# A two-layer hybrid trunk on one core: the second layer's pieces put in rounds of 1/32 head, a memset moved to VectorE, and sums of squares moved to another PSUM bank

## The chip, the cores and the metric

The kernel runs on one core of one Trainium2 chip. The metric is device time in microseconds (us) for one launch. PE is TensorE, DVE VectorE, ACT ScalarE, POOL GpSimd, SP the engine that issues the DMAs. Each engine works through its own queue in order.

## The reference, cut to what matters

640 tokens (128 of a prompt, 512 latent) go through two layers of width 1024. Layer A is a gated chunk mixer, layer B a gated DeltaNet scanned in both directions. Cut to layer B, whose order is changed:

```python
qkv, z, ab = split(h @ w_in)                  # per head: k 128, q 128, v 256, z 256 columns
qkv = silu(short_conv(qkv, conv_w))           # 5 taps over the tokens
q = l2norm(q) * 128**-0.5;  k = l2norm(k)     # l2norm needs the sum of squares of each token
# per head, per direction, in chunks:
A   = strict_lower(kb @ k.T * decay)
sol = (I + A)^-1 [v*beta, kb*exp(gcum)]       # triangular solve inside a chunk
S, o = scan over the chunks                   # 128x256 state from chunk to chunk
y = rmsnorm(o_fwd + o_bwd) * norm_g * silu(z)
out = y @ w_out
```

## The kernel before

Tokens are five tiles of 128 (`TT = 5`, tile 0 is the prompt). All large products are done as three products of high and low parts (`mm3`, lines 230 to 232); weights come through the queue `ws`, are cast to a high part on ACT (line 225), and the low part is subtracted on POOL or DVE (line 226).

Layer B goes head by head, eight heads. What it does is written as Python generators, and each `yield` ends a piece:

- `project_head` and `project_z`: 16 pieces each, every piece one `mm3` of 128x320 into a bank of the pool `pp` (two banks), so three matmuls a piece;
- `conv` (lines 834 to 842): on DVE four taps over 642 columns (L837) and a last product (L842), on ACT the first tap and a tanh written over `xp`. `gap` (L848) then sets the two columns between prompt and latent tokens to zero again;
- `post_k`, `post_q`, `post_v`: sums of squares, transposes through `flip` (L235, into the pool `px`, which has one bank), copies out of it on ACT (L901, L927). `post_q` takes q's sums of squares with matmuls against a column of ones (L858, also into `px`), and DVE copies them out (L912);
- `chunk`: the triangular inverse in three groups of token tiles, (0), (1, 4), (2, 3), started 0.09 of a head apart, 40 pieces each. Six levels of doubling: L1006 on PE, a masked product Y on DVE (L1011), L1017 and L1018 on PE, a copy TU on ACT (L1021). Then `U16`, half of it written by POOL (L1030), is transposed by L1037, refined through L1046, L1047, and used by L1053. The result goes through L1063 to G. All small products share the pool `pt` (three banks);
- `scan`: the recurrence, L1101 then L1104 and L1109 on DVE, L1114 and L1115, L1129, with the pool `ps` (two banks);
- `norm_o`, `gate_z` (transposes of o by `flip` into `px`, product on DVE L1196) and `residual` (lines 682 to 690: a load, three POOL products and a store, in windows of four heads).

`stages` gives each generator a stretch of time, in heads. `turns` spreads its pieces evenly over that stretch and sorts all pieces by their time; the program is written in that order. From time 0 on, where the first scan begins, PE and SP keep the written order (`manual_schedule`); the orders of DVE, ACT and POOL are made by a scheduler from the same pieces. A tile of PSUM whose bank is still being read makes the next writer of that bank wait.

Of the kernel before, what the change touches and what calls it, by code (L numbers as in the profile page):

```python
# [13 lines left out]
P = 128  # L14
# [4 lines left out]
NPR = 128  # L19
NSA = 512  # L20
NT = NPR + NSA
TT = NT // P
# [51 lines left out]
def tok(c):  # L74

    s = 0 if c == 0 else 2 + c * P
    return slice(s, s + P)


ZW, ZPOS = (1, 2, 3, 4, 5, 6, 6, 6), 0  # L80
START = 2, 0.3, 1
PIECES = {"scan": 24, "chunk": 40, "norm_o": 4, "gate_z": 4, "conv": 8, "post_k": 13,
          "post_q": 7, "post_v": 5, "gates": 7, "gates_e": 26, "residual": 16}


def stages():
# [5 lines left out]
    for w in range(-2, H + 1):  # L92
        at = lambda d: 0 <= w + d < H
        add = lambda f, arg, t0, t1, k=None: parts.append((f, arg, k or PIECES[f], w + t0, w + t1))
        slots = [("head", w + 2, q) for q in range(4) if at(2)]
        slots[ZPOS:ZPOS] = [("z", h, q) for h in range(H) if ZW[h] == w for q in (4, 5)]
        start = START[w + 2] if w + 2 < len(START) else 0
        wide = (n - start) / len(slots) if slots else 0
# [27 lines left out]

def turns(parts):

    return sorted((f + (k + 0.5) / n * (t - f), i) for i, (_, _, n, f, t) in enumerate(parts)
                  for k in range(n))  # L130


class Stream:
# [69 lines left out]
class Trunk:  # L203
# [8 lines left out]
    def t(self, pool, shape, dt, tag, bufs=None):  # L212
        kw = {} if bufs is None else {"bufs": bufs}
        return pool.tile(shape, dt, tag=tag, name=self.name(tag), **kw)
# [407 lines left out]
    def layer_b(self):  # L622
# [6 lines left out]
        with contextlib.ExitStack() as banks, pool("b_c") as bc:  # L629
# [19 lines left out]
            with pool("b_1", 1) as self.b1, pool("b_2", 2) as self.b2, contextlib.ExitStack() as self.last:  # L649
                self.bg = self.last.enter_context(pool("b_g", 1))  # L650
                self.xp = [t(self.b1, [P, NT + 6], F32, f"xp{i}") for i in range(2)]
                for x in self.xp:
                    nc.gpsimd.memset(x, 0.0)
                self.nxp = 0
                self.kq, self.ch, self.oo, self.ssq, self.acc, self.zz = {}, {}, {}, {}, {}, {}
                parts = stages()
                gens = [getattr(self, f)(*arg) for f, arg, *_ in parts]
                order = turns(parts)
                manual = [when >= 0 for when, _ in order].index(True)
                for _, i in order[:manual]:  # L660
                    next(gens[i], None)

                with tc.manual_schedule(engines=MANUAL):
                    for _, i in order[manual:]:
                        next(gens[i], None)
                    for g in gens:
                        for _ in g:
                            pass
                self.last.close()
                self.out_b()  # L670
# [174 lines left out]
        yield  # L845

    def gap(self, xp):
        self.nc.gpsimd.memset(xp[:, 2 + NPR : 4 + NPR], 0.0)  # L848

    def squares(self, s, xp, dst):  # L850

# [52 lines left out]
    def post_q(self, h, q):  # L904

        nc, t = self.nc, self.t
        s, xp = self.acc[h, q]
        kq = self.kq[h]
        ssq = self.ssq[h] = t(self.b1, [P, TT], F32, "ssq", bufs=5)
        px = self.bank("px", [P, 4, P])  # L910
        yield from self.squares(s, xp, px[:, 0, 0:TT])
        nc.vector.tensor_copy(ssq, px[:, 0, 0:TT])  # L912
        yield
        s4 = s[:, tok(1).start : tok(4).stop].rearrange("p (c n) -> p c n", c=4)
        nc.scalar.copy(kq[:, 1:TT, 1, :], s4)
        yield
        nc.scalar.copy(kq[:, 0, 1, :], s[:, tok(0)])
        yield
# [484 lines left out]
```

## Time and profile before

| | |
|---|---|
| times of three runs | 1387.90, 1391.88 and 1399.34 us, median 1391.88 |
| the profiled execution | 1387.0 us, span 1385.2 us |
| PE busy | 1296.3 us, 94% of the span |
| DVE, ACT, POOL busy | 869.8, 578.4 and 548.0 us |
| mean granted PE clock | 0.977 |

Layer A and its output product take the span up to about 545 us. Layer B's early projections and gates follow to about 690 us, the steady heads to about 1180 us, then the last head and the output product. A busy PE row counts a matmul's whole stay in the array, and rows overlap; where start times stand in a timeline, the distance from start to start is the matmul's price. In a row `<-` names the releaser of the wait, as the profile infers it.

### The profile page before, as it was taken

Reading aid. Unit: us, or ns where it says so; the run is one execution under the profiler, and the core shown is the slowest. Engines: PE = TensorE matmul, PEld = TensorE weight load, DVE = VectorE, ACT = ScalarE, POOL = GpSimd, SP = SyncE. Lnnn points to the kernel's source line nnn. Section 1 sums busy time; section 2 is a strip of 40 time slices with the busy share of each in tenths; the row PEclk is TensorE's granted clock in tenths of the full one; section 3 lists DMA queues with packets and bytes.
Section 4 is the critical chain, followed back from the end, with each engine's and each line's share of the span. In section 5 each row is a group of like instructions: output and inputs, shape, how many; then the busy total and the mean of one; then the engine's idle time right before and its main releaser. Section 6 shows DMA issues by size and latency. Waiting matters only on the chain.

```text
span 1385.2 us, 22850 instructions
## 1 busy us (share of the span) xinstructions
PE 1296.3 (94%) x8773; PEld 1148.0 (83%) x8773; DVE 869.8 (63%) x1572; ACT 578.4 (42%) x1352; POOL 548.0 (40%) x592
## 2 busy tenths in 40 slices
PE   7999999999999998888899999899898998999995
PEld 4688999999997876778788989899898988987784
DVE  4654744444448646987777676687766777455447
ACT  2333522223224325656454554545446354343320
POOL 0221322122126315453546354474655656431014
PEclk9999999999999999999999999999999999999998
DMA  8522233333336232231322224233342432435731
GB/s 329 164 71 82 96 128 117 134 122 122 124 127 252 76 103 108 79 114 57 103 72 69 93 72 136 60 108 109 90 139 68 130 120 66 151 131 159 258 97 77
DMA packets 90255, 163.18 MB, mean 118 GB/s; under 512 B 9089, under 2 KB 55457, under 8 KB 90017
## 3 DMA queue, kind: packets, MB, share of 16 engines
q1 hardware_dynamic: 90144, 161.71, 35.4%
q8 instruction: 69, 1.13, 0.3%
q14 instruction: 42, 0.34, 0.1%
HBM read 135.97 MB, written 25.71 MB: 117 GB/s over the span
## 4 chain that ended last, share of the span: by engine, by line
PE 65%; DVE 14%; issue 6%; POOL 5%; DMA 4%; ACT 4%; SPq 0%; POOLq 0%; DVEq 0%; ACTq 0%
PE pacc L230 10%; PE pacc L232 10%; PE pacc L231 10%; PE pp L230 6%; PE pp L231 6%; PE pp L232 6%; DVE cacc L837 3%; PE ps L1101 3%; DVE M L971 3%; POOL rs L243 2%; PE ps L1115 2%; PE pmod L302 2%; PE pacc L452 1%; POOL wlo L226 1%; DMA lnb<-in_ln 1%
## 5 line engine op out<-in xcount | busy, mean ns | idle before, releaser
L226 POOL TENSOR_TENSOR wlo<-wraw,whi 128x256 fp32r<-128x256 f32 (+1 forms) x193 | 200.3, 1057 | 232.4 <-ACT whi L225 213.5
L230 PE MATMUL pp<-hThi,whi 128*128 128x320 f32 (+1 forms) x784 | 284.7, 363 | 1.5 <-ACT hThi L225 1.5
L231 PE MATMUL pp<-hThi,wlo 128*128 128x320 f32 (+1 forms) x784 | 247.2, 315 | 0.0
L232 PE MATMUL pp<-hTlo,whi 128*128 128x320 f32 (+1 forms) x784 | 246.8, 315 | 0.2 <-DVE hTlo L226 0.2
L225 ACT CAST whi<-wraw 128x256 fp32r<-128x256 f32 (+1 forms) x268 | 147.5, 594 | 101.6 <-PE pacc L231 66.5
L837 DVE SCALAR_TENSOR_TENSOR cacc<-xp,convw,cacc 128x642 f32<-128x642 f32 x128 | 144.2, 1127 | 24.5 <-ACT cacc L834 22.8
L230 PE MATMUL pacc<-hThi,whi 128*128 128x320 f32 x512 | 159.6, 312 | 0.0
L232 PE MATMUL pacc<-hTlo,whi 128*128 128x320 f32 x512 | 158.3, 309 | 0.0
L231 PE MATMUL pacc<-hThi,wlo 128*128 128x320 f32 x512 | 158.2, 309 | 0.0
L230 PEld LDWEIGHTS pp<-hThi,whi 128*128 128x128 f32 (+1 forms) x784 | 151.1, 193 | 5.8 <-ACT hThi L225 1.8
L231 PEld LDWEIGHTS pp<-hThi,wlo 128*128 128x128 f32 (+1 forms) x784 | 150.9, 192 | 4.5
L232 PEld LDWEIGHTS pp<-hTlo,whi 128*128 128x128 f32 (+1 forms) x784 | 149.7, 191 | 1.7 <-DVE hTlo L226 0.6
L226 DVE TENSOR_TENSOR wlo<-wraw,whi 128x1024 fp32r<-128x1024 f32 (+1 forms) x75 | 87.6, 1173 | 69.6 <-ACT whi L225 69.4
L230 PEld LDWEIGHTS pacc<-hThi,whi 128*128 128x128 f32 x512 | 96.1, 188 | 3.1 <-issue 2.2
L231 PEld LDWEIGHTS pacc<-hThi,wlo 128*128 128x128 f32 x512 | 96.1, 188 | 0.0
L232 PEld LDWEIGHTS pacc<-hTlo,whi 128*128 128x128 f32 x512 | 96.1, 188 | 0.0
L243 POOL TENSOR_TENSOR rs<-ve,mhalf 128x1 f32<-128x1 f32 (+2 forms) x39 | 39.6, 1017 | 141.0 <-DVE ve L241 141.0
L251 POOL TENSOR_SCALAR gsq<-gsq 128x320 f32<-128x320 f32 (+1 forms) x52 | 27.7, 532 | 136.9 <-ACT gsq L250 135.9
L252 DVE TENSOR_TENSOR gsq<-pacc,gsq 128x320 f32<-128x320 f32 (+1 forms) x52 | 29.1, 564 | 73.0 <-POOL gsq L251 72.9
L230 PE MATMUL pacc<-whi,hThi 128*128 128x512 f32 x160 | 63.2, 406 | 8.2 <-ACT whi L225 4.8
L250 ACT ACTIVATE gsq<-pacc 128x320 f32<-128x320 f32 (+1 forms) x52 | 25.7, 498 | 106.9 <-PE pacc L232 102.9
L1101 PE MATMUL ps<-S,kq 128*128 128x256 f32 x256 | 64.2, 390 | 4.6 <-DVE o L1129 4.6
(323 smaller groups left out, 3001.1 us busy)
## 6 DMA issues: line engine op xcount, KB each, us to landing
wraw<-in_w_b SPq DMA_DIRECT2D x48, 512.0 KB
wraw<-in_w_ada SPq DMA_DIRECT2D x37, 512.0 KB
wraw<-in_w_uz SPq DMA_DIRECT2D x32, 512.0 KB
v<-kvd SPq DMA_DIRECT2D x72, 128.0 KB
wraw<-in_a_wo SPq DMA_DIRECT2D x16, 512.0 KB
wraw<-in_b_wo SPq DMA_DIRECT2D x16, 512.0 KB
kvd<-nat SPq DMA_DIRECT2D x24, 320.0 KB
cacc<-yd SPq DMA_DIRECT2D x24, 320.0 KB
```

Of the source, the lines that this page charges most:

```text
L225: self.nc.scalar.copy(hi, src)
L226: (e_lo or self.nc.vector).tensor_tensor(lo, src, f32(hi), op=ALU.subtract)
L230: mm(out, l_hi, r_hi, start=start, stop=False)
L231: mm(out, l_lo, r_hi, start=False, stop=False)
L232: mm(out, l_hi, r_lo, start=False, stop=stop)
L243: nc.gpsimd.tensor_tensor(r, ve, self.mhalf[:, 0:n], op=ALU.pow)
L252: nc.vector.tensor_tensor(sq, u, sq, op=ALU.mult)
L302: nc.tensor.matmul(ps[32 * j : 32 * j + 32, 0:256], self.sil[:, 4 * i + j, :], w[:, j, :], start=(i == 0), stop=(i == 1), tile_position=(0 ...
L837: nc.vector.scalar_tensor_tensor(acc, xp[:, i : i + PADN], w[:, i : i + 1], acc, op0=ALU.mult, op1=ALU.add)
L971: nc.vector.scalar_tensor_tensor(M[:, i, 1 + d], pe[:, i], self.beta[:, c, d, h : h + 1], m[:, 2 + d], op0=ALU.mult, op1=ALU.mult)
L1101: nc.tensor.matmul(p[:, q], kq[:, c, q, :], S, start=True, stop=True)
L1115: nc.tensor.matmul(p[:, 1], G[:, 1 + d], r, start=True, stop=True)
```

## The change

`turns` cuts time into rounds of 1/32 head. Within a round the projections come first, then `chunk`, then everything else, then `scan`; inside each class the old order holds. Times below 0 keep the old order. Second, `gap` is issued on VectorE instead of GpSimd. Third, `post_q` puts its sums of squares into a bank of `pt` instead of `px`. Nothing is computed differently.

```diff
+ROUNDS = 32
 ...
 def turns(parts):
-    return sorted((f + (k + 0.5) / n * (t - f), i) for i, (_, _, n, f, t) in enumerate(parts)
-                  for k in range(n))
+    rank = lambda f: 0 if f.startswith("project_") else {"chunk": 1, "scan": 3}.get(f, 2)
+    order = [(f + (k + 0.5) / n * (t - f), i) for i, (_, _, n, f, t) in enumerate(parts) for k in range(n)]
+    return sorted(order, key=lambda x: (x[0] * ROUNDS // 1, rank(parts[x[1]][0]), x) if x[0] >= 0 else (x[0] * ROUNDS,))
 ...
     def gap(self, xp):
-        self.nc.gpsimd.memset(xp[:, 2 + NPR : 4 + NPR], 0.0)
+        self.nc.vector.memset(xp[:, 2 + NPR : 4 + NPR], 0.0)
 ...
-        px = self.bank("px", [P, 4, P])
-        yield from self.squares(s, xp, px[:, 0, 0:TT])
-        nc.vector.tensor_copy(ssq, px[:, 0, 0:TT])
+        ps = self.bank("pt", [P, TT])
+        yield from self.squares(s, xp, ps)
+        nc.vector.tensor_copy(ssq, ps)
```

Line numbers of the changed kernel are higher by 3 from `turns` on (L858 is L861 there, L235 is L238).

The first place is PE's queue at the sums of squares of a middle head: `L858` and the projections up to `L1053`. Before:

```order
L235 MATMUL px_9331<-ident_487,nat_9072 128x128
L858 MATMUL px_9282<-ones_4857,xp_763_4879 128x1 x5
L230 MATMUL pp_9267<-hThi_64,whi_9179 128x320
L231 MATMUL pp_9267<-hThi_64,wlo_9180 128x320
L232 MATMUL pp_9267<-hTlo_65,whi_9179 128x320
L230 MATMUL pp_9267<-hThi_64,whi_9179 128x320
L231 MATMUL pp_9267<-hThi_64,wlo_9180 128x320
L232 MATMUL pp_9267<-hTlo_65,whi_9179 128x320
L1053 LDWEIGHTS U_1684_9220
```

The same place in the changed kernel; nine of the twelve projection matmuls are shown, and three more and then `L1056` (L1053 before) follow:

```order
L238 MATMUL px_9338<-ident_487,nat_9091 128x128
L861 MATMUL pt_9308<-ones_4857,xp_763_4879 128x1 x5
L233 MATMUL pp_9243<-hThi_64,whi_9169 128x320
L234 MATMUL pp_9243<-hThi_64,wlo_9170 128x320
L235 MATMUL pp_9243<-hTlo_65,whi_9169 128x320
L233 MATMUL pp_9351<-hThi_64,whi_9169 128x320
L234 MATMUL pp_9351<-hThi_64,wlo_9170 128x320
L235 MATMUL pp_9351<-hTlo_65,whi_9169 128x320
L233 MATMUL pp_9351<-hThi_64,whi_9169 128x320
L234 MATMUL pp_9351<-hThi_64,wlo_9170 128x320
L235 MATMUL pp_9351<-hTlo_65,whi_9169 128x320
```

The sums now go to `pt`, and twelve projection matmuls instead of six stand between them and `L1053`.

The second place is PE's queue where `gate_z` begins, in the changed kernel: the last transpose of `post_v` (out of `cacc`) and the first four of `gate_z` (out of `o`), both into the one bank of `px`.

```order
L234 MATMUL pp_8628<-hThi_64,wlo_8446 128x320
L235 MATMUL pp_8628<-hTlo_65,whi_8445 128x320
L238 MATMUL px_8654<-ident_487,cacc_8361 128x128
L238 MATMUL px_8656<-ident_487,o_7483 128x128
L238 MATMUL px_8656<-ident_487,o_7686 128x128
L238 MATMUL px_8656<-ident_487,o_7690 128x128
L238 MATMUL px_8656<-ident_487,o_7487 128x128
L233 MATMUL pp_8628<-hThi_64,whi_8445 128x320
```

Before, six projection matmuls stood between the two; now none does. The same happens at six heads.

The third place is POOL's queue at `U16` of the third group, with the semaphores waited for. Before:

```order
L226 TENSOR_TENSOR wlo_9382<-wraw_9065,whi_9381 128x256 [waits Activation_49] x3
L682 TENSOR_SCALAR lnb_9479<-lnb_9479 128x512 [waits DMAHW6_49]
L687 TENSOR_TENSOR rn_9482<-rn_9482,lnb_9479 128x256 [waits DMAHW7_49,Pool_49]
L689 TENSOR_TENSOR rn_9482<-rn_9482,lnb_9479 128x256 [waits Pool_49]
L1030 TENSOR_SCALAR U_1711_9334<-TU_1580_8715 128x2x2x64 [waits PE_49]
L848 MEMSET xp_762_4878 128x2 [waits DVE_49]
```

And in the changed kernel:

```order
L229 TENSOR_TENSOR wlo_9362<-wraw_9059,whi_9361 128x256 [waits Activation_49] x3
L685 TENSOR_SCALAR lnb_9505<-lnb_9505 128x512 [waits DMAHW6_49]
L690 TENSOR_TENSOR rn_9508<-rn_9508,lnb_9505 128x256 [waits DMAHW7_49,Pool_49]
L692 TENSOR_TENSOR rn_9508<-rn_9508,lnb_9505 128x256 [waits Pool_49]
L1033 TENSOR_SCALAR U_1710_9334<-TU_1580_8715 128x2x2x64 [waits PE_49]
```

The memset behind `U16` has gone; the residual's three products ahead of it have stayed.

Over the stretch from the first scan to the last, PE changes from a small 16-bit matmul (L991 to L1053) to a projection 118 times before and 54 times now, and from any small matmul to a projection 290 times before and 198 times now.

## The prediction

> **What bounds the kernel now.** I read the page's first part, then the busy time by stage, since layer A is not touched.
>
> ```profile
> PE 1296.3 (94%) x8773; PEld 1148.0 (83%) x8773; DVE 869.8 (63%) x1572; ACT 578.4 (42%) x1352; POOL 548.0 (40%) x592
> core 0: us, PE busy (x) PEld busy (x) DVE busy (x) ACT busy (x) POOL busy (x), PEclk, DMA share, GB/s
> 690.00:1180.00 490.00, 465.59 (x3621) 431.40 (x3620) 354.98 (x688) 248.85 (x703) 275.75 (x340) 0.97 0.31 96
> ```
>
> PE is the bound. In the steady heads, 690 to 1180 us, it is idle for 490 - 465.6 = 24.4 us, and its clock is 0.97. The stage before 690 is written in the old order, so what rounds can win lies in these 24.4 us, in the clock, and in how cheaply PE goes from one kind of matmul to the next. PE's waits there, in total, with their number and the longest, are:
>
> ```profile
> PE pt L1037 <- POOL xp L848: 12.2, 6, 2.9
> PE ps L1101 <- DVE o L1129: 4.6, 6, 1.2
> PE px L858 <- ACT kq L901: 4.1, 5, 1.1
> PE pt L1018 <- DVE Y L1011: 2.2, 5, 0.4
> PE pt L1017 <- DVE Y L1011: 1.1, 1, 1.1
> ```
>
> Two of them carry names that the change touches: L858 waits for its bank in `px`, and L1037 waits for what looks like the memset. PE's timeline at one head shows both, and what follows them:
>
> ```profile
> 805.12 0.27 PE L235 MATMUL px<-ident,nat 128*128 128x128 f32 x1
> 805.89 1.28 PE L858 MATMUL px<-ones,xp 128*128 128x1 f32 x10 [0.50 <-ACT kq L901]
> ...
> 807.99 0.40 PE L1053 MATMUL pt<-R,U 128*128 128x128 f16 x4
> 809.54 0.61 PE L1037 MATMUL pt<-id,U 128*128 128x128 f16 x4 [1.15 <-POOL xp L848]
> 810.32 0.47 PE L231 MATMUL pp<-hThi,wlo 128*128 128x320 f32 x1
> 810.59 0.47 PE L232 MATMUL pp<-hTlo,whi 128*128 128x320 f32 x1
> ```
>
> After the two waits the projections start 0.27 us apart.
>
> **Memset.** L1037 does not wait for the memset. The U16 of the third group may be written only when L1053 of the second group has read the old one (one buffer), L1037 is the next thing in PE's queue, and POOL does this between the two:
>
> ```profile
> 890.23 0.62 POOL L682 TENSOR_SCALAR lnb<-lnb 128x512 f32<-128x512 f32 x1 [1.24 <-DMA lnb<-in_ln]
> 890.93 1.17 POOL L687 TENSOR_TENSOR rn<-rn,lnb 128x256 f32<-128x256 f32 x1
> 892.18 0.72 POOL L689 TENSOR_TENSOR rn<-rn,lnb 128x256 f32<-128x256 f32 x1
> 892.99 0.40 POOL L1030 TENSOR_SCALAR U<-TU 128x256 f16<-128x256 f16 x1
> 893.33 0.10 POOL L848 MEMSET xp<- 128x2 f32 x1
> ```
>
> U16 (L1030) ends at 893.39, the memset at 893.43: the memset stands behind what PE needs. In four heads the residual's products, held by a load, are ahead; in the others U16 alone. The order shows all of this unchanged but for the memset, so I leave the 12.2 us in place: term **0**, ends -0.6 (0.1 us at each of six) and -12.2. On DVE the memset's nearest rows are POOL's own and DVE's copy of five columns:
>
> ```profile
> L848 POOL MEMSET xp<- 128x2 f32 x24 | 2.4, 99 | 11.3 <-DVE cacc L842 9.4 <-ACT xp L854 1.9
> L912 DVE COPY ssq<-px 128x5 f32<-128x5 f32 x6 | 1.0, 160 | 1.8 <-PE px L858 1.7
> L837 DVE SCALAR_TENSOR_TENSOR cacc<-xp,convw,cacc 128x642 f32<-128x642 f32 x96 | 108.7, 1132 | 23.4 <-ACT cacc L834 21.8
> ```
>
> There are 32 of them (three convolutions and one square a head): at most 32 x 0.16 = 5.1 us of DVE, which has 490 - 355 = 135 us free in the steady heads. After a convolution the memset follows DVE's own L842 and waits for nobody; after `squares` it waits for ACT's square, and behind it stands L912's copy, which needs that square too. Term 0, at worst 5.1 us if DVE's cover were gone. POOL loses a wait (11.3 us of idling before L848) that no PE row names except as above.
>
> **Sums of squares to `pt`.** L858 no longer waits for L901's copy: 4.1 us in five heads. But in the four heads with a residual PE then only comes sooner to L1037, whose wait POOL ends: there the gain is taken back. I keep the one without, 0.5 us (the row at 805.89). Term **-0.5**, ends 0 and -4.1. In `pt` the sums hold one of three banks until DVE's L912; behind L858 twelve projection matmuls follow in the middle heads before `pt` is used again, and L912 takes 0.16 us.
>
> **Rounds: a new neighbour in `px`.** At six heads `gate_z`'s first transposes now stand directly behind `post_v`'s last, in the same bank, and wait for ACT's copy out of it. This is not in the trace; the nearest thing is L858 above, a transpose, an ACT copy of 128x128, then the next writer:
>
> ```profile
> L901 ACT COPY kq<-px 128x128 f32<-128x128 f32 x6 | 1.5, 246 | 1.3 <-PE px L235 1.3
> L927 ACT ACTIVATE nat<-px 128x128 f32<-128x128 f32 x12 | 3.2, 267 | 0.0
> ```
>
> The copies are alike (246 and 267 ns), so I take the mean wait of L858, 4.1 / 5 = 0.82 us: six times **+4.9 us**, ends 0 (PE held up by something else anyway) and 6 x 1.1 = 6.6. One wait in `px` is exchanged for another.
>
> **Rounds: fewer changes of kind.** What a change costs stands in PE's timeline:
>
> ```profile
> 800.38 0.28 PE L1006 MATMUL pt<-TU,A 128*128 128x64 f16 x4
> 800.49 0.39 PE L230 MATMUL pp<-hThi,whi 128*128 128x320 f32 x1
> 800.72 0.31 PE L231 MATMUL pp<-hThi,wlo 128*128 128x320 f32 x1
> 800.87 0.31 PE L232 MATMUL pp<-hTlo,whi 128*128 128x320 f32 x1
> ```
>
> The first projection behind 16-bit matmuls holds the next for 0.23 us, the second for 0.15: 0.08 us a change. There are 118 - 54 = 64 fewer: **-5.1 us**. Behind 32-bit matmuls the first holds longer still,
>
> ```profile
> 827.09 0.59 PE L1114 MATMUL ps<-v,G 128*128 128x256 f32 x2
> 827.52 0.59 PE L1115 MATMUL ps<-v,G 128*128 128x256 f32 x2
> 827.77 0.49 PE L230 MATMUL pp<-hThi,whi 128*128 128x320 f32 x1
> 828.10 0.31 PE L231 MATMUL pp<-hThi,wlo 128*128 128x320 f32 x1
> ```
>
> 0.33 us, but nothing is lost: two such matmuls take 0.43 us from start to start (827.09 to 827.52), so the L1115 would reach 827.95; L230 begins 0.18 before that and ends its hold 0.15 after it, as long as any projection. Ends: 0, and all 290 - 198 = 92 changes at 0.33 - 0.15 = 0.18, -16.6 us.
>
> **Rounds: shorter cover.** A chunk's PE step needs DVE's or ACT's answer to the one before. Projections between them hide it. The longest such run grows, but the shortest shrinks: where L1018 follows L1006 at the last level, twelve projections and four transposes stood between, now six projections, 6 x 0.15 = 0.9 us. Counting the order with such start-to-start times, no step of `chunk` behind the first scans had a cover under 1.5 us; now 20 places do. What the answer takes when DVE is free:
>
> ```profile
> 867.24 0.47 PE L1006 MATMUL pt<-TU,A 128*128 128x64 f16 x10
> 867.51 0.95 DVE L1011 TENSOR_TENSOR Y<-pt,wm 128x128 f16<-128x128 f32 x3 [0.51 <-PE pt L1006]
> 869.83 0.23 PE L1018 MATMUL pt<-TU,Y 128*128 128x128 f16 x1
> ```
>
> All three Y are there at 868.46; L1006's ten starts (0.3 us), a change of kind (0.08) and six projections would bring PE to about 868.5. It just fits. Term 0; the upper end is the slower rival. The waits of L1101 and L1018 (6.8 us) I leave: ends -6.8 and 0.
>
> **The clock.** The granted clock was half of full in these stretches:
>
> ```profile
> 809.60:812.80 3.20, 3.20 (x14) 3.19 (x15) 0.22 (x1) 0.58 (x1) 1.16 (x1) 0.50 0.03 5
> 891.50:898.10 6.60, 4.65 (x18) 4.30 (x19) 1.04 (x3) 0.58 (x1) 2.92 (x5) 0.50 0.01 2
> ...
> sum 26.40, PE 20.39 PEld 19.50 DVE 3.04 ACT 3.82 POOL 11.15; mean PE 4.08 PEld 3.90 DVE 0.61 ACT 0.76 POOL 2.23
> ```
>
> Five heads, 20.4 us of PE at half speed, at most 10.2 us lost. Each stretch begins in the wait of L1037 or at its end, behind L858's one-column matmuls. At 809.6 three light pieces led up to it, waits of 0.50 and 1.15 us and L858's 1.28. The change puts six more projections (0.88 us) between L858 and L1037, but lets L1037's wait grow by what L858 lost. Term 0, ends -10.2 and +5.
>
> The Trainium skill bears on this ("TensorE: Matmul & The Clock Gate", Part 1): PE is taken to half clock after about 3.4 us without work, and gaps below that are harmless. By that rule no wait here would cost clock, the term would be 0 at both ends and the sum -0.7 us whatever the waits do. The trace disagrees: half clock followed waits of 0.50 and 1.15 us; by it the sum can lie between -10.9 and +4.3 us by this term alone.
>
> **The sum**: -0.5 + 4.9 - 5.1 = -0.7 us. The profiled execution took 1387.0 us, less than all three runs shown; the middle of the four times is (1387.9 + 1391.9) / 2 = 1389.9. I set the sum against that: **1389 us**. Against 1387.0 it would be 1386.
>
> **The rivals.** Differences under 1% (13.9 us) are about what a measurement of this kernel cannot tell from none.
>
> - *Slower, by late answers.* At the 20 places DVE takes one more L837 (1.13 us) before Y or T32, with some 0.3 us of slack: 20 x 0.8 = +16 us, 1405. It decides when DVE still has such a tap in hand as L1006 ends. For it: DVE is 72% busy there, and L1018 already waits 0.4 us in five heads. Against it: the free DVE in the rows at 867. Chance 0.20.
> - *Faster, by the clock.* If L858 and L1037 are now far enough apart that the clock holds, and their waits do not merge, 10.2 us and L858's other 3.6 go: 1389 - 14 = 1375. For it, the first head, where L1037 waited with no L858 close by:
>
> ```profile
> 729.35 0.34 PE L1037 MATMUL pt<-id,U 128*128 128x128 f16 x3 [0.88 <-POOL xp L848]
> ```
>
> ```profile
> 728.00:735.00 7.00, 6.12 (x50) 5.65 (x49) 3.46 (x8) 4.32 (x15) 1.97 (x4) 1.00 0.00 0
> ```
>
> The clock stayed whole. Against it: 0.88 us is short, and with the residual the longest wait is 2.9. Chance 0.15.
> - *Faster, by the memset.* Were the profile's name right and L1037 held by L848, 12.2 and 10.2 us would go: 1366. Against it stands the POOL order. Chance 0.07.
> - *Faster, by the changes of kind at their upper end*: -16.6 + 4.9 - 0.5 = -12, with a wait of L1018 or two gone 1375. Chance 0.05.
>
> **How the numbers follow.** My forecast, within 1% with everything nearly cancelling, has 0.53. Slower by over 1% has the first rival's 0.20 and 0.01 for a clock that falls more often; faster by over 1% the other three less a part that stays inside, 0.26. The range runs from just inside the clock rival with the waits of L1018 gone (1389 - 14 - 5 = 1370) to the slower rival with a little clock (1406).
>
> **What would show it.** L858's wait gone from PE's waits; a new wait of a transpose L238 on ACT's copy L930, six times, near 0.8 us; L1040 (L1037 before) still waiting for POOL 12 us or more; PE busy in the steady heads lower by about 5 us; half-clock stretches still once a head behind L1040. Wrong would be: L1040's wait much shorter, no half clock in the middle heads, or waits of L1020 and L1021 on DVE above 5 us in sum.

## The result, and the profile after

The changed kernel took 1429.49 us (median of four, 1429.37 to 1434.58) against 1391.85 us before: ratio 1.0271, 95% interval 1.0247 to 1.0295. It is **2.7% slower, 38 us**. The forecast was 1389 us with 1406 as the upper end, so it was wrong. The profiled execution took 1429.5 us with a span of 1427.7, 42.5 us longer than the span of before; its page has:

```profile
PE 1313.2 (92%) x8773; PEld 1161.4 (81%) x8773; DVE 870.0 (61%) x1604; ACT 574.9 (40%) x1352; POOL 549.5 (38%) x560
```

PE is busy 17 us longer, with the same 8773 matmuls, and still fills less of the span. A fair comparison takes the same work on both sides: from the 529th matmul of layer B's projections to the 2257th, which is six heads; 38.3 of the 42.5 us lie in it. The busy time for that stretch, first of before, then of after:

```profile
703.28:1206.10 502.82, 478.41 (x3727) 443.38 (x3726) 358.13 (x701) 250.90 (x709) 282.07 (x350) 0.97 0.33 102
```

```profile
709.28:1250.40 541.12, 493.04 (x3727) 455.15 (x3726) 354.94 (x721) 248.67 (x712) 284.55 (x325) 0.94 0.30 93
```

The columns are the stretch, its length, and the busy time of PE, PE's loads, DVE, ACT and POOL, then PE's granted clock. PE is idle for 48.1 us instead of 24.4, and the clock falls from 0.97 to 0.94. The stretches of half clock (a granted clock of 0.50) in these heads are eleven instead of five; here are the third and the sum over all, then the sum over the five of before:

```profile
849.38:856.21 6.83, 4.95 (x14) 3.96 (x14) 4.68 (x13) 0.47 (x1) 4.69 (x6) 0.50 0.03 11
...
sum 64.86, PE 55.70 PEld 48.59 DVE 24.86 ACT 8.32 POOL 33.13; mean PE 5.06 PEld 4.42 DVE 2.26 ACT 0.76 POOL 3.01
```

```profile
sum 27.31, PE 20.95 PEld 19.99 DVE 3.45 ACT 4.00 POOL 11.48; mean PE 4.19 PEld 4.00 DVE 0.69 ACT 0.80 POOL 2.30
```

55.7 us of PE at half speed lose 27.9 us; before it was 20.95 us and 10.5. (The prediction's 20.4 and 10.2 came from windows a little narrower than the stretches.) So the 38.3 us of these six heads split, with rounding, into 23.7 us of new idling, 17.4 us of clock, and -2.7 us that is left over (465.2 instead of 467.9 us of work at full clock). The waits of PE from 690 to 1230 us:

```profile
PE pt L1009 <- DVE TU L996: 24.7, 6, 4.3
PE pt L1040 <- POOL U L1033: 13.7, 6, 5.0
PE px L238 <- ACT kq L904: 4.3, 2, 2.2
PE pt L1040 <- ACT U L1030: 2.4, 5, 0.5
PE px L238 <- ACT nat L930: 2.2, 6, 0.4
PE pt L1020 <- DVE Y L1014: 0.7, 1, 0.7
```

One row carries nearly all: once a head the first level of group (0)'s inverse, L1009, waits 4.1 us for DVE's product TU. Before, the same step, L1006, had no such wait in these heads. PE's timeline at one head of after, without the projections that stand between the rows:

```profile
844.23 0.28 PE L994 MATMUL pt<-id,A 128*128 128x128 f16 x2
...
845.29 0.60 PE L238 MATMUL px<-ident,cacc 128*128 128x128 f32 x4
...
846.90 0.31 PE L235 MATMUL pp<-hTlo,whi 128*128 128x320 f32 x1
851.26 0.26 PE L1009 MATMUL pt<-TU,A 128*128 128x64 f16 x2 [4.05 <-DVE TU L996]
```

and the same head before:

```profile
829.72 0.28 PE L991 MATMUL pt<-id,A 128*128 128x128 f16 x2
...
831.65 1.03 PE L1101 MATMUL ps<-S,kq 128*128 128x256 f32 x4
833.40 1.13 PE L1101 MATMUL ps<-S,kq 128*128 128x256 f32 x4 [0.72 <-DVE o L1129]
...
834.82 0.23 PE L1006 MATMUL pt<-TU,A 128*128 128x64 f16 x2
```

Before, scan's L1101 stood between L991 and L1006, and the second four of it waited for DVE's `o`. After, `chunk` has a rank ahead of `scan`, so L1009 comes first and the L1104 behind it. From L991 to L1006 PE took 5.10 us; from L994 to the end of the last projection ahead of L1009 it takes 847.21 - 844.23 = 2.98. What DVE does meanwhile, after and then before:

```profile
844.85 1.77 DVE L966 SCALAR_TENSOR_TENSOR A<-ge,beta,masks 128x128 f32<-128x128 f32 x4
846.53 4.01 DVE L974 SCALAR_TENSOR_TENSOR M<-pe,beta,masks 128x128 f32<-128x128 f32 x4
850.47 0.41 DVE L1132 TENSOR_TENSOR o<-o,ps 128x256 f32<-128x256 f32 x1
850.80 0.41 DVE L996 TENSOR_TENSOR TU<-pt,wm 128x256 f16<-128x256 f32 x1
```

```profile
829.09 1.12 DVE L963 SCALAR_TENSOR_TENSOR A<-ge,beta,masks 128x128 f32<-128x128 f32 x4
830.13 2.88 DVE L971 SCALAR_TENSOR_TENSOR M<-pe,beta,masks 128x128 f32<-128x128 f32 x3
832.94 0.41 DVE L1129 TENSOR_TENSOR o<-o,ps 128x256 f32<-128x256 f32 x1
833.27 0.91 DVE L971 SCALAR_TENSOR_TENSOR M<-pe,beta,masks 128x128 f32<-128x128 f32 x1
834.10 0.41 DVE L993 TENSOR_TENSOR TU<-pt,wm 128x256 f16<-128x256 f32 x1
```

TU itself takes 0.4 us; ahead of it stand A and M of the **next** group, 6 us. TU ended 4.79 us behind the start of L991 before, and ends 6.98 us behind L994 after, because DVE begins A 1.25 us later against PE (why was not followed), and A and M take 0.9 us longer. The cover is 2.1 us shorter, the answer 2.2 us later, and 0.3 us was spare: 4.0 us.

Much of M's 4.0 us goes together with POOL's work in the same stretch, first below. Four of the same products later in the same trace, where POOL is idle, are in the second fence:

```profile
846.70 1.31 POOL L980 TENSOR_TENSOR A<-A,ident 128x512 f16<-128x512 f32 x1 [0.22 <-DVE A L966]
848.09 1.15 POOL L982 TENSOR_TENSOR L<-A,A 128x512 f16<-128x512 f32 x1
849.20 1.20 POOL L997 TENSOR_TENSOR TU<-A,wm 128x512 f16<-128x512 f16 x1
```

```profile
923.79 1.14 DVE L974 SCALAR_TENSOR_TENSOR M<-pe,beta,masks 128x128 f32<-128x128 f32 x4 [1.04 <-PE pt L1066]
```

The first of the four at 846.53 takes 0.26 us from start to start; the three behind it take 1.28, 1.23 and 1.16, and each ends 0.14 or 0.15 us behind one of POOL's three products; it is so in all six heads. So of DVE's queue ahead of TU some 2.9 us go with POOL's work at the same time. It was nearly so before (3.8 us for the four, at 830.13 and 833.27). No run moved POOL's products, so this is read from the traces alone.

### The profile page after: what moved, and what is told of

Its sections match the earlier page's. It is cut to its first block, busy times and chain, and to the rows that moved or that the text cites. A ratio compares the mean times of both kernels' runs of the same rounds, so it can differ in the third digit from the quotient of the medians.

```text
span 1427.7 us, 22870 instructions
## 1 busy us (share of the span) xinstructions
PE 1313.2 (92%) x8773; PEld 1161.4 (81%) x8773; DVE 870.0 (61%) x1604; ACT 574.9 (40%) x1352; POOL 549.5 (38%) x560
## 4 chain that ended last, share of the span: by engine, by line
PE 66%; DVE 17%; issue 5%; POOL 4%; DMA 4%; ACT 2%; SPq 0%; POOLq 0%; DVEq 0%; ACTq 0%
PE pacc L233 10%; PE pacc L235 10%; PE pacc L234 10%; PE pp L233 6%; PE pp L235 6%; PE pp L234 6%; DVE cacc L840 4%; PE ps L1104 4%; DVE M L974 3%; POOL rs L246 2%; PE pmod L305 2%; DVE A L966 1%; PE pacc L455 1%; PE ps L1118 1%; PE px L238 1%
## 5 line engine op out<-in xcount | busy, mean ns | idle before, releaser
L229 POOL TENSOR_TENSOR wlo<-wraw,whi 128x256 fp32r<-128x256 f32 (+1 forms) x193 | 205.1, 1081 | 226.5 <-ACT whi L228 202.9
L233 PE MATMUL pp<-hThi,whi 128*128 128x320 f32 (+1 forms) x784 | 275.5, 351 | 1.5 <-ACT hThi L228 1.5
L235 PE MATMUL pp<-hTlo,whi 128*128 128x320 f32 (+1 forms) x784 | 248.0, 316 | 0.2 <-DVE hTlo L229 0.2
L235 PE MATMUL pacc<-hTlo,whi 128*128 128x320 f32 x512 | 158.3, 309 | 0.0
L235 PEld LDWEIGHTS pp<-hTlo,whi 128*128 128x128 f32 (+1 forms) x784 | 150.6, 192 | 1.7 <-DVE hTlo L229 0.6
L840 DVE SCALAR_TENSOR_TENSOR cacc<-xp,convw,cacc 128x642 f32<-128x642 f32 x128 | 140.2, 1095 | 16.5 <-ACT cacc L837 15.4
L235 PEld LDWEIGHTS pacc<-hTlo,whi 128*128 128x128 f32 x512 | 96.1, 188 | 0.0
L1104 PE MATMUL ps<-S,kq 128*128 128x256 f32 x256 | 70.7, 425 | 0.0
```

The lines of the kernel that those rows point to most:

```text
L229: (e_lo or self.nc.vector).tensor_tensor(lo, src, f32(hi), op=ALU.subtract)
L233: mm(out, l_hi, r_hi, start=start, stop=False)
L235: mm(out, l_hi, r_lo, start=False, stop=stop)
L840: nc.vector.scalar_tensor_tensor(acc, xp[:, i : i + PADN], w[:, i : i + 1], acc, op0=ALU.mult, op1=ALU.add)
L1104: nc.tensor.matmul(p[:, q], kq[:, c, q, :], S, start=True, stop=True)
```

## The experiments

Each is the changed kernel with one edit, unless it says otherwise. "Six heads" means the stretch above, split as above.

### The rounds, or the rest

`e1_no_rounds` takes `ROUNDS` and the new `turns` out:

```diff
-    order = [... rank(...) ...]
+    return sorted((f + (k + 0.5) / n * (t - f), i) for i, ...)
```

> The change without its rounds: the memset on VectorE and the sums of squares in pt, in the old order. Theory A (the rounds cost the 38 us: in them chunk stands ahead of scan, L1009 loses the cover that scan's L1104 gave it): within 5 us of before, 1387 to 1397, L858 (L861 after) waits for nothing, no wait of L1009 above 1 us, half clock once a head. Theory B (the memset in VectorE's queue makes VectorE late for TU): a good part of the 38 us stays, 1405 to 1430, with L1009 waiting for VectorE.

`e2_rounds_only` is the kernel before with the new `turns` alone.

> The rounds alone: memset on GpSimd, sums of squares in px. Theory A: all of the slowdown is here, 1425 to 1440 (the sums in px wait for kq's copy besides, up to 4 us), L1009 waits some 4 us once a head. Theory B: near before, 1390 to 1400.

Measured: 1390.61 us, ratio 0.9991 (0.9973 to 1.0009), and 1434.74 us, ratio 1.0309 (1.0288 to 1.0331). The cost is the rounds'. Without them the two other edits cost nothing, and the memset's name is gone from the wait while the wait stays (`e1_no_rounds`):

```profile
PE pt L1037 <- POOL U L1030: 16.7, 6, 4.2
PE ps L1101 <- DVE o L1129: 5.5, 6, 1.2
```

What L858 no longer waits there, L1037 waits longer (17.8 instead of 12.8 us, with ACT's part). With the rounds alone it is the other way round: L861 (L858 before) waits 12.2 us, far more than the 4 us expected, and L1040 6.1 us.

### The ranks of chunk and scan

```diff
-    {"chunk": 1, "scan": 3}.get(f, 2)
+    {"chunk": 3, "scan": 1}.get(f, 2)
```

> The change with scan ahead of the others and chunk last within a round (ranks 1 and 3 exchanged), so that scan's four L1104 stand between L994 and the first L1009 of the last group once more. Theory A: the waits of L1009 fall from 24.7 us to under 8 us (four L1104 give 1.6 us of the 4.1 and hold PE until DVE's o besides), and with them the half clock behind them: 1390 to 1405. Rival C (any order with nine projections in a row at the head of a round starves the chunk's steps): the waits move to other steps of chunk, 1415 to 1430.

Measured: 1390.15 us, ratio 0.9999 (0.9974 to 1.0024). Theory A. Rounds of 1/32 with nine projections at their head do not cost 38 us; the order of `chunk` and `scan` in them does. L1009's wait is down to a third (8.5 us, where under 8 was expected), and what the prediction feared shows in its place, L1021 behind a late Y:

```profile
PE pt L1021 <- DVE Y L1014: 9.5, 7, 1.9
PE pt L1009 <- DVE TU L996: 8.5, 6, 2.0
```

`e6_flat` keeps the projections first and drops the other ranks:

```diff
-    rank = lambda f: 0 if f.startswith("project_") else {"chunk": 1, "scan": 3}.get(f, 2)
+    rank = lambda f: 0 if f.startswith("project_") else 1
```

> Rounds with the projections first and all else in its old order (no ranks for chunk and scan). Theory A: L1104 stands ahead of the first L1009 again; time near the version with scan first, 1385 to 1397, with waits of L1009 of 1.0 to 1.5 us a head. Rival C: 1405 or more.

Measured: 1382.29 us, ratio 0.9938 (0.9914 to 0.9962): 0.6% faster than before, below what theory A gave. In the six heads (494.4 us) PE idles 24.8 us, as before; half clock costs 3.4 instead of 10.5 us, and there is 1.8 us less of work. So "projections first" alone was a small gain, also against the 1390.61 us without rounds, and the ranks behind it threw it away.

### One piece moved

`e9_one_piece` moves the single piece with that L1009, and with it its Y on DVE, behind its round's scan; L956 and everything else stay.

```diff
+    late = lambda i, k: parts[i][0] == "chunk" and parts[i][1][1] == GROUPS[0] and k in (8, 9)
-    rank = lambda f: 0 if ...
+    rank = lambda i, k: 4 if late(i, k) else 0 if ...
```

> The change with one piece of its order moved, once a head: the first L1009 of group (0) stands behind the L956 and the four scan matmuls L1104 of its round instead of ahead of them (on VectorE its Y moves with it); everything else stays. Theory A (this one place holds the cost): the wait goes from 4.1 us to about 4.1 - 0.9 - 1.9 = 1.3 us a head, 17 us of waiting gone, and with it the half clock behind it (about 2.5 us of loss a head in the last four heads): 25 to 32 us gone, 1397 to 1405. Rival C (the waits come with the rounds wherever chunk stands): under 10 us gone.

Measured: 1402.83 us, ratio 1.0104 (1.0048 to 1.0160), 27 us less than the change. One piece a head holds that much. But not for the reason given: the waiting did not go, it was divided (lines are higher by 3 again):

```profile
839.17 1.13 PE L1107 MATMUL ps<-S,kq 128*128 128x256 f32 x4 [2.03 <-DVE o L1135]
840.13 0.22 PE L1012 MATMUL pt<-TU,A 128*128 128x64 f16 x2
...
842.81 0.22 PE L1023 MATMUL pt<-Y,TU 128*128 128x64 f16 x2 [1.06 <-DVE Y L1017]
```

PE now meets the same stretch of DVE at scan's `o`, 2.0 us, and at Y, 1.1 us. In the six heads idling falls only from 48.1 to 41.1 us; the loss by clock falls from 27.9 to 12.8. Two short waits, 3.1 us together, cost far less clock than the long one of 4.1 us.

### DVE's queue

`e8_M_short` leaves PE's order alone and shortens what stands ahead of TU: one product in place of four for the second group. It leaves the factor beta out, so what this kernel computes is not the layer any more; its time alone counts here.

```diff
+        if cs == GROUPS[1]:
+            nc.vector.tensor_tensor(M[:, :, 1:3], pe[...], m[...], op=ALU.mult)
...
+                if cs != GROUPS[1]:
                     nc.vector.scalar_tensor_tensor(M[:, i, 1 + d], pe[:, i], self.beta[...], ...)
```

> The change with the second group's four products into M on VectorE (L974, 1.0 us each, the last thing ahead of TU in VectorE's queue) replaced by one product of 128x512 that leaves the factor beta out; PE's order is the change's. Theory A' (the wait of L1009 is VectorE's queue, not TU's own work and not GpSimd): one product of some 1.2 us instead of four of 4.0: the wait falls by 2.8 us a head to about 1.3 (17 us), and with the clock 22 to 30 us are gone, 1399 to 1408. Rival E (TU waits for PE's L994 or for the bank, VectorE's queue only stands beside it): the wait stays over 3 us and the time over 1420.

Measured: 1392.54 us, ratio 1.0007 (0.9986 to 1.0028). The whole loss is gone, more than expected, since the product took 0.68 us and not 1.2:

```profile
833.57 1.80 DVE L966 SCALAR_TENSOR_TENSOR A<-ge,beta,masks 128x128 f32<-128x128 f32 x4
835.29 0.68 DVE L973 TENSOR_TENSOR M<-pe,masks 128x512 f32<-128x512 f32 x1
835.90 0.41 DVE L1136 TENSOR_TENSOR o<-o,ps 128x256 f32<-128x256 f32 x1
836.23 0.41 DVE L1000 TENSOR_TENSOR TU<-pt,wm 128x256 f16<-128x256 f32 x1
```

```profile
PE pt L1013 <- DVE TU L1000: 4.8, 6, 1.0
```

A is as slow as in the change; M alone is short, and L1009 (L1013 here) waits 0.8 us. In the six heads 17.2 us of idling and 15.6 us of clock go. Of the 4.1 us of waiting, 3.3 are these M products in DVE's queue. Whether by their own work or by POOL's products between them the run does not tell apart, since one product leaves fewer places for POOL's to come between.

`e4_M_later` was meant as the same test by order: the four M products written behind TU.

> The change with chunk's products into M (L974, four of 1.0 us on VectorE) written behind the product into TU (L996) instead of ahead of it; PE's order is as in the change. Theory A in its form 'L1009 waits for VectorE's queue, of which M is 4 us': the wait of L1009 goes from 4.1 us a head to about 0, with the half clock behind it (3.4 to 5 us of PE at half speed, 1.7 to 2.5 us lost a head): 30 to 40 us gone, 1390 to 1400. Rival D (VectorE's backlog only moves on to Y L1014 and r L1107, for which L1020 and L1118 wait): 1415 to 1430 with new waits of L1020 or L1117.

Measured: 1416.01 us, ratio 1.0174 (1.0157 to 1.0191), with 20.6 us of waiting at L1009 left. The time is in theory D's range, but the new waits that D names are not there (0.7 us at L1020). The edit did not have the effect it was meant for: DVE's order is made by a scheduler, and that put M ahead of TU again (L998 is M, L994 TU here):

```profile
836.75 1.86 DVE L998 SCALAR_TENSOR_TENSOR M<-pe,beta,masks 128x128 f32<-128x128 f32 x2
838.53 0.41 DVE L1134 TENSOR_TENSOR o<-o,ps 128x256 f32<-128x256 f32 x1
838.87 2.13 DVE L998 SCALAR_TENSOR_TENSOR M<-pe,beta,masks 128x128 f32<-128x128 f32 x2
840.92 0.41 DVE L994 TENSOR_TENSOR TU<-pt,wm 128x256 f16<-128x256 f32 x1
```

Where its 13 us come from was not followed further; in the six heads there is 4.7 us less idling and 6.2 us less loss by clock.

### The clock by itself

`e7_filler` fills the wait with useless work and takes no wait away:

```diff
+            if l == 1 and nt == 1 and h > 1:
+                for _ in range(17):
+                    nc.tensor.matmul(fill, self.id16, self.wm[:, 0:2]..., start=True, stop=True)
```

> The change with 17 useless 16-bit matmuls of 512 columns (the identity against a mask) ahead of the first L1009 of group (0) in the six steady heads, into the bank that L1009 then writes; nothing else moves on PE or VectorE. An estimate from L994's 128 columns in 0.056 us: 0.22 us each, 3.8 us of work in the 4.1 us of waiting. Theory F (the half clock behind L1009 follows PE's idleness there, and costs 10 us or so by itself): the wait is filled, the clock holds behind it, and the time falls by 8 to 14 us, 1416 to 1421, though PE has 22 us more to do. Rival G (the half clock has another cause, the light 16-bit pieces or VectorE's lateness): the time stays within 3 us of the change's 1429, and the half clock behind L1009 too.

Measured: 1411.91 us, ratio 1.0156 (1.0118 to 1.0194): **17.6 us faster than the change with 22 us more work for PE.** The stretch about the filled wait runs at full clock here, as in all six heads, where the change had half:

```profile
841.80 3.84 PE L1011 MATMUL pt<-wm,id 128*128 128x512 f16 x17
846.05 0.22 PE L1014 MATMUL pt<-TU,A 128*128 128x64 f16 x2 [0.41 <-DVE TU L997]
```

```profile
845.50:852.50 7.00, 6.59 (x44) 5.80 (x42) 4.78 (x14) 1.52 (x4) 5.77 (x7) 1.00 0.00 1
```

In the six heads idling falls by 21.2 us, the work grows by 23.1, and the loss by clock falls from 27.9 to 9.4. That is theory F, with a size nearly twice as large as expected. In the change the six stretches behind L1009 hold 25.4 us of PE at half speed, so 12.7 us of the loss: PE's idleness of 4.1 us costs about 2 us of clock a head on top of itself. The other 5.7 us are gone from stretches behind other waits, and no run shows why.

### What else holds PE, and other rounds

`f3_flat_U` is the flat version with U's half written by DVE; `f4_before_U` is the same edit on the kernel before.

```diff
-        nc.gpsimd.tensor_scalar(half(U16[:, 64 : W - 64], 0), ...)
+        nc.vector.tensor_scalar(half(U16[:, 64 : W - 64], 0), ...)
```

> The flat rounds, with U's half (L1033) written by VectorE instead of GpSimd. Theory H (L1040 waits for U's half because it stands in GpSimd's queue behind the residual's products, as the prediction read it): L1040's waits fall from 10.4 us to 6 x 0.5 = 3 us, the last half-clock stretch of the steady heads goes, VectorE takes some 0.2 to 0.4 us a group more: 6 to 9 us faster than flat, 1373 to 1378. Rival I (L1040 then waits as long for VectorE, behind a tap of 1.1 us or more): within 3 us of flat, 1380 to 1386.

> The kernel before with U's half (L1030) on VectorE and nothing else; the memset stays on GpSimd. Theory H (L1037 waits for U's half in GpSimd's queue, not for the memset behind it): L1037's wait falls from 12.8 us to 3 to 7 us (VectorE has a tap in hand now and then) and the half clock behind it mostly goes: 8 to 15 us faster, 1376 to 1383. Rival J (the profile's name is right, the memset L848 holds L1037): the wait and the time stay, 1388 to 1394.

Measured: 1370.78 us, ratio 0.9863 (0.9839 to 0.9886), and 1385.04 us, ratio 0.9962 (0.9948 to 0.9976). The flat version gains 11.5 us by it, more than theory H gave, and is the fastest here, 1.4% faster than before: in its six heads no half clock is left and 18.7 us of idling. The wait itself fell less than H said, from 10.4 to 7.5 us with ACT's part; L1021's wait for Y fell as well, from 5.2 to 1.9 us. In both the wait passes in part to DVE; first the flat version, then the kernel before:

```profile
PE pt L1040 <- DVE U L1033: 6.8, 5, 1.7
PE pt L1009 <- DVE TU L996: 5.2, 6, 1.3
```

```profile
PE pt L1037 <- DVE U L1030: 6.4, 5, 2.0
PE px L858 <- ACT kq L901: 5.2, 5, 2.1
```

On the kernel before the wait falls from 12.8 to 7.6 us with ACT's part, but half clock still costs 10.9 us, so that it gains 5.7 us, short of the 8 expected. With the memset still on POOL, this also rules out rival J. L858's wait is still there ahead of it.

The flat rounds at other sizes, `ROUNDS` 64 and 16:

> Flat rounds of 1/64 head. Theory A (what counts is what stands between a step of chunk and the step that needs its answer; halving the rounds gives back the finer mix): between before and the flat rounds of 1/32, 1380 to 1392, no wait of L1009 above 1.5 us. Rival C (long runs of projections are what helps): the gain over before is lost, 1390 to 1395.

> Flat rounds of 1/16 head: about eighteen projections at the head of a round and, behind them, twice as many of chunk's steps with no projection in between. Theory A: the cover between a step and its answer is gone in many places, waits of L1020, L1021 and L1009 for VectorE above 30 us in sum and half clock behind them, 1410 to 1460. Rival C (long runs of projections are what helps): faster than flat rounds of 1/32, 1372 to 1382.

Measured: 1392.73 us, ratio 1.0017 (1.0000 to 1.0034), and 1396.52 us, ratio 1.0041 (1.0024 to 1.0057). With 64 the time is in rival C's range and just above theory A's; L1009 waits 4.1 us in all and never above 1.3, as theory A said, but L1040 now waits 15.5 us for POOL and half clock costs 13.3 us. With 16 the time is in neither range: rounds twice as long are not faster, against C, and theory A's collapse did not come: L1020, L1021 and L1009 wait 3.7 us in all, other steps wait instead,

```profile
PE pt L1066 <- DVE T L1059: 13.2, 9, 2.3
```

idling is 38.3 us in the six heads and half clock costs 6.8. So neither theory covers both sizes. That the gain of the flat 1/32 is a matter of where single pieces fall, and not of the size of a round, is our reading; no run isolates it.

## Why the prediction was wrong

**The step that failed** is "shorter cover", set to 0. Its mechanism, a late answer of DVE to a step of `chunk`, is what happened, but it looked in the wrong places. It counted the places with a cover under 1.5 us, and took the answer's time from a row where DVE was free. L1009's cover fell from 5.1 to 3.0 us: far above 1.5, so it was not in the list. The answer there takes 7 us, since A and M of the next group stand ahead of TU. `e8_M_short` shows M in that queue to be 3.3 of the 4.1 us of waiting, and `e9_one_piece` that this place alone holds most of the 38 us (27). The upper end of the term, +16 us, was too small for the same reason; the slower rival named Y, L1018 and T32, and the waits of L1020 and L1021 on DVE that were to show it came to 0.7 us.

The trace of before had a sign that was read as a harmless term: the waits of L1101 for `o` (4.6 us), which it left as they were. `o` stands in the middle of those M products. PE already ran into the same stretch of DVE there, and at L1006 only 0.3 us was spare: what the ranks took from the cover beyond that was paid in full.

**The clock** was 0, with +5 as its end; it was +17.4 us. That term was tied to the wait of L1037 alone. It should have been tied to each new wait.

Point by point, the rest:

- *Memset*: right. 0 by `e1_no_rounds`; L1040's wait stayed (16.1 us with both rows, 12.8 before), and `f4_before_U` shows that it follows U, not the memset, as POOL's order said.
- *Sums of squares to `pt`*: L858's wait is gone, as said, and L1040's is longer, as said too.
- *New neighbour in `px`*: there, six times, but 0.37 us each and not 0.82: 2.2 instead of 4.9 us. Not foreseen was a second one in `px`: in two heads kq's second flip waits 2.1 us for ACT's first copy out of the bank, which stands on ACT behind a product that waits for a load:

```profile
817.07 0.40 ACT L977 ACTIVATE M<-kn,scal 128x128 f32<-128x128 f32 x1 [2.88 <-DMA kn<-kvd]
817.38 0.56 ACT L904 COPY kq<-px 128x512 f32<-128x512 f32 x1
```

- *Fewer changes of kind*: -5.1 us forecast. Work at full clock fell by 2.7 us in the six heads, but by 1.2 us already in `e1_no_rounds`, which has no rounds, and by as much by the rounds alone (`e2_rounds_only`). At most some 1.5 us are left for this term, and no run shows that they come from it: the sign may be right, the size was over three times too large.
- *Half clock once a head behind L1040*: no. It comes behind L1009 in all six heads, and behind L1040 or the new wait of L238 as well in five.

## What to carry to other kernels

Cover is worth what the answering engine's queue asks, not what the answer takes when that engine is free: for each step whose cover shrinks, add up what stands ahead of the answer in that queue, the next group's work too. A wait of a few tenths in the trace of before can mark a place without slack: here all but 0.3 us of the lost cover and the later answer came back as waiting. And a long wait costs PE's clock besides; somewhat less waiting in two parts, or the same wait filled with useless work, was much cheaper.

## What the runs showed of the hardware

- Every stretch of half clock in these traces but the last of each, which runs to the end of the kernel, is 3.41 us long or a whole multiple (6.83, 10.24). In the change, half clock came with the six waits of 4.0 to 4.3 us each time; it followed the six waits of 2.0 to 2.3 us at scan's `o` in `e9_one_piece` twice, and the six of 0.75 to 1.0 us at L1013 in `e8_M_short` never. The Trainium skill ("TensorE: Matmul & The Clock Gate", Part 1) has a free-running window of about 3.4 us, and half clock after an idle one: the lengths agree with it, but not all of the beginnings. In three of the six heads of the change the clock fell 2.2 to 2.4 us into the wait, before PE had been idle for a whole window, and the two behind waits of 2.0 to 2.3 us had no such window either. The prediction took from this page of the Trainium skill that shorter gaps are harmless; these runs do not bear it out.
- DVE's products into A took 1.12 us for four with POOL idle (before, at 829.09) and 1.77 us beside POOL's products of `norm_o` (after, at 844.85). Four into M took 1.14 us with POOL idle (after, at 923.79) and 4.01 us beside three POOL products of 1.15 to 1.31 us (after, at 846.53), three of them ending as one of POOL's ended. The traces show the two side by side; that an engine off the critical path made the one on it slower is read from that, and no run changed POOL's work alone.
